# Early-stage work of a hybrid attention / Hyena / expert kernel placed on other engines: split subtractions, one modulation and half of a spectrum

## The chip, the cores and the metric

One NeuronCore of a Trainium2 chip runs the whole program. The metric is device microseconds for one execution. The kernel before took 1320.08 us (median of 3 runs, 1317.94 to 1324.70). The profile is of another execution, which took 1325.77 us.

## The reference, cut to what matters

One layer over 512 latent tokens of width 1024, with 256 context tokens:

```python
sh1, sc1, g1, sh2, sc2, g2 = adaln(c, w_mod, b_mod)          # silu(c) @ w_mod + b_mod
h  = modulate(rmsnorm(x, norm1_g), sh1, sc1)                   # h * (1 + scale) + shift
q, k, v, hy_in, cf_in = jnp.split(h @ w_in, splits, axis=-1)
hc = modulate(rmsnorm(ctx, norm1_g), csh1, csc1)               # only its k and v are used
attn = neighbourhood_attention(q, k, v, kc, vc, rpb)
hy   = hyena_mixer(hy_in, ...)      # short conv, then two gated long convolutions
cf   = conformer_conv(cf_in, ...)   # GLU, 31-tap depthwise conv, layer norm, silu
x = x + g1 * (concat([attn, hy, cf]) @ w_out)
x = x + g2 * expert_choice_ffn(modulate(rmsnorm(x, norm2_g), sh2, sc2), ...)   # 16 experts
return rmsnorm(x, final_norm_g)
```

The long convolutions of Hyena need filter spectra. The filters come from a small sine network over the 512 positions, and depend on no token:

```python
h = jnp.sin(fr * (z @ w1 + b1)); h = jnp.sin(fr * (h @ w2 + b2))
h = (h @ w3).reshape(L, 2, HY_ORDER, D_HY) * exp(-t * rate)
k_spec = jnp.fft.rfft(concat([fwd, 0, reversed(bwd[1:])]), axis=0)
```

The experts' weights are 384 MB of the 458 MB that the kernel moves.

## The kernel before, in words

**Buffers.** Large data lives in 24 buffers of 128 x 2048 floats, taken with `U(name)`. A counter `used` follows the program text: `free(k, keep)` and `free_only(k)` lower it, and `pump(keep)` (lines 72 to 74) places further loads from one long list as long as `used < 24 - keep`. Each load is one DMA on SyncE's queue, in the order of that list.

**Split products.** The projections run with operands split into two parts: `hi` is the value rounded to float32r by a ScalarE copy, `lo` is the remainder from a subtraction. `mm3` (line 547) then makes three products of 512 columns: hi·hi (line 548), lo·hi or hi·lo (549 and 550). `split` (line 510) does this for a weight buffer of 2048 columns in four slices of 512: the copy on ScalarE (line 515), the subtraction on VectorE or GpSimd (line 516); `DVE_LO` (line 491) lists which slices of which weight buffer go to VectorE. The first weights, `('hy1', 0)`, are not in the list, so all four of their subtractions are GpSimd's.

**The filter.** `filt_layer` (lines 294 to 309) is one sine layer: two products, then seven VectorE operations on each half and a ScalarE sine. The last layer's weights `fw3` are split beforehand (lines 316 to 319): the 512-column part's subtraction on VectorE, the 1024-column part's on GpSimd. `filt_out` (line 356) multiplies and applies the decay.

**The spectrum.** `spectrum` (line 383) is a generator of four steps: two over the even lags (lines 389 to 398), which make KE, and two over the odd lags (lines 399 to 411), one for each half of the frequencies. A step over the odd lags has four float32 products of 512 columns (line 406, two instructions each in the trace), two ScalarE copies with a scale (407) and four VectorE operations (409, 410), which make KP and KM. When it ends it gives back three buffers (line 412).

**Modulated x.** `modulate_split` (line 494) takes the eight 128 x 512 tiles of the transposed, normalized x in two halves of four: each is scaled and shifted (line 504, VectorE), copied to `hi` (line 505, ScalarE), and after the four come the four subtractions (line 507); the string `pool` says which tiles' subtractions are GpSimd's: here tiles 3 and 7.

**Order.** Lines 531 to 543 are a block in which TensorE, ScalarE and VectorE keep the order of the program text. A string spells it out: `a` is a step of adaln group 0 (eight steps of products with w_mod, then the row's copy, then transposes and the making of `A1` and `B1`), `F` filt_out, `s` a step of the spectrum, `T` a step of the transposes of x, `W` the split of the first projection weights, `h` and `M` the steps of modulate_split. Everything outside the block, projections, Hyena, conformer convolution, is put in order by a planner at build time, which simulates the engines from costs of its own and takes ready work in order of the program text; there the string at line 823 (`.` is one k of a projection: three products; other letters are steps beside it) gives the text order, which the planner may depart from. PSUM tiles of `psA` are four in number; the spectrum's steps and the projections both use them.

Of the kernel before, what the change touches and what calls it, by code (L numbers as in the profile page):

```python
# [9 lines left out]
FT = mybir.dt.float32  # L10
# [3 lines left out]
AF = mybir.ActivationFunctionType  # L14
OP = mybir.AluOpType
# [35 lines left out]
def hybrid_kernel(ctx: ExitStack, tc: tile.TileContext, a, out: bass.AP):  # L51
    nc = tc.nc
# [12 lines left out]
    def U(name, dt=FT):  # L65
        used[0] += 1
        assert used[0] <= NU, name
        return big.tile([128, 2048], dt, name=name, tag="U")
# [14 lines left out]
    def psA(name="psA"):  # L83
        return psum.tile([128, 512], FT, name=name, tag="A", bufs=4)
# [36 lines left out]
    A1 = small.tile([128, 2, 8], FT, name="A1")  # L121
    B1 = small.tile([128, 2, 8], FT, name="B1")
# [69 lines left out]
    v512 = lambda t: t.rearrange("p (k n) -> p k n", n=512)  # L192
# [93 lines left out]
    fw3 = take("fw3")  # L286
# [7 lines left out]
    def filt_layer(dst, m, w, rhs, b):  # L294

        ps, arg, n = psA("pF"), W("arg")[m], W("nper")[m]
        hs = [slice(0, 256), slice(256, 512)]
        for h in hs:
            mm(ps[m, h], w, rhs[:, h], start=True, stop=True)
        for h in hs:  # L300
            x_, n_ = arg[:, h], n[:, h]
            nc.vector.tensor_scalar(x_, ps[m, h], b[m], ffr[m], op0=OP.add, op1=OP.mult)
            nc.vector.tensor_scalar(n_, x_, 1.0 / TWO_PI, MAGIC, op0=OP.mult, op1=OP.add)
            nc.vector.tensor_scalar(n_, n_, MAGIC, None, op0=OP.subtract)

            for cst in (C_HI, C_LO):
                nc.vector.scalar_tensor_tensor(x_, n_, -cst, x_, op0=OP.mult, op1=OP.add)
            nc.vector.tensor_scalar(x_, x_, 3.1415925, -3.1415925, op0=OP.min, op1=OP.max)
            nc.scalar.activation(dst[m, h], x_, AF.Sin)


    fsd = fw3[:, 1024:2048]
    nc.gpsimd.tensor_add(fsd[:, 0:512], fw3[:, 0:512], fw3[:, 512:1024])
    nc.gpsimd.tensor_sub(fsd[:, 512:1024], fw3[:, 512:1024], fw3[:, 0:512])
    fw3s = [U("fw3s", FR) for _ in range(2)]
    for n, src in ((0, fsd), (1, fw3[:, 0:512])):
        w = src.shape[1]
        nc.scalar.activation(fw3s[n][:, 0:w], src, AF.Copy)
        (nc.vector if n else nc.gpsimd).tensor_sub(fw3s[n][:, 1024:1024 + w], src, fw3s[n][:, 0:w].bitcast(FT))
    h1 = W("h1")  # L320
    h2f = W("h2f")
    filt_layer(h1, slice(64, 128), p1[0:33, P1["fw1"]], dz[0:33, 1024:1536], fb1)
    filt_layer(h2f, slice(0, 128), dz[64:128, 1024:1152], h1[64:128], fb2)

    fst = U("fst", FR)
    h2s = fst[:, 0:512]
# [5 lines left out]
    hr = [U("hr0"), U("hr1")]  # L332
# [155 lines left out]

    ADA_KEEP = [7, 4, 2, 0]
    KEEP = {'hy1': 8, 'hy0': 7, 'cf': 10, 'q': 8, 'v': 7}  # L490
    DVE_LO = {('q', 0): (0, 2), ('q', 1): (1, 3), ('k', 1): (0, 1), ('k', 0): (2, 3), ('cf', 1): (0, 1), ('hy0', 1): (2, 3), ('cf', 0): (1, 3), ('hy0', 0): (0, 2)}
    ADA = [(4, 0), (4, 4), (2, 8), (2, 10)]

    def modulate_split(src, n, v, name, pool="01010101"):

        nu = (8 * n) // 2048
        hi = [U(name + "h", FR) for _ in range(nu)]
        lo = [U(name + "l", FR) for _ in range(nu)]
        per = 2048 // n
        at = lambda t, k: t[k // per].rearrange("p (k n) -> p k n", n=n)[:, k % per]  # L500
        yield (lambda k: at(hi, k)), (lambda k: at(lo, k))
        for h in range(2):
            for k in range(4 * h, 4 * h + 4):
                nc.vector.tensor_scalar(src(k), src(k), A1[:, v, k:k + 1], B1[:, v, k:k + 1], op0=OP.mult, op1=OP.add)
                nc.scalar.activation(at(hi, k), src(k), AF.Copy)  # L505
            for k in range(4 * h, 4 * h + 4):
                (nc.gpsimd if pool[k] == "1" else nc.vector).tensor_sub(at(lo, k), src(k), at(hi, k).bitcast(FT))  # L507
            yield

    def split(raw, keep, dve=()):  # L510
        hi = U("wh", FR)
        lo = U("wl", FR)
        for i in range(4):
            s = slice(i * 512, (i + 1) * 512)
            nc.scalar.activation(hi[:, s], raw[:, s], AF.Copy)  # L515
            (nc.vector if i in dve else nc.gpsimd).tensor_sub(lo[:, s], raw[:, s], hi[:, s].bitcast(FT))  # L516
        free(1, keep)
        return hi, lo
# [5 lines left out]
    def next_split():  # L524
        c, u = splits.popleft()
        presplit[c, u] = split(take(("win", c, u)), KEEP[c], DVE_LO.get((c, u), ()))

    hmod = modulate_split(lambda k: v512(hr[k // 4])[:, k % 4], 512, 0, "h", "00010001")
    ada0, spec, xt = adaln(0), spectrum(), x_transposed()
    E_ = mybir.EngineType  # L530
    with tc.manual_schedule(engines={E_.PE, E_.Activation, E_.DVE}):
        for w in "aFaasTsaTaTsTaaaaaWhMMs":
            if w == "F":
                filt_out()
            elif w == "W":
                next_split()
            elif w == "h":
                hh, hl = next(hmod)
            else:
                next({"a": ada0, "s": spec, "T": xt, "M": hmod}[w], None)  # L540
        for g in (xt, spec, ada0, hmod):
            for _ in g:
                pass
    free_only(2)
# [225 lines left out]
    def finish(*gens):  # L770
        for g in gens:
            for _ in g:
                pass
# [35 lines left out]
    side = {"h": hyena(), "m": adaln(1), "n": adaln(2), "c": conv_cf(), "x": ctx_prep()}  # L809
    side["s"] = (next_split() for _ in range(9))  # L810

    def projections():
        for c in "hy1 hy0 cf q v".split():
            yield from {"hy1": lambda: project("hy1", 2, lambda m, ps: evac_hy(m + 4, ps)), "hy0": lambda: project("hy0", 4, evac_hy),
                        "cf": lambda: project("cf", 4, evac_cf, [2, 3, 0, 1]), "q": lambda: project("q", 4, evac_q),
                        "v": lambda: project("v", 4, evac_v, ctx_part=ctx_v)}[c]()


    side["."] = projections()
    with ExitStack() as ordered:  # L820
        if False:
            ordered.enter_context(tc.manual_schedule(engines={E_.PE}))
        for w in "......s.............h............hh.......m...hm..h...h....m..m..h...h..h...h...m....hh..........h.m...mm..hh...n.h.h....h..c....m..xcnh..n..hh..m....c....c..n..c.sxn.m....c.c.c........c..c..x..c.....cc.....c........cccccccccccc":
            next(side[w], None)
        finish(side["."], *[side[w] for w in "hmncx"])
    finish(ln_cf())
    vblk = lambda c: vv[:, c // 16] if c % 16 == 0 else vo[:, c // 16]

# [25 lines left out]
    for u in range(2):  # L854
        parts.append([t.rearrange("p (k n) -> p k n", n=512) for t in split(take(("win", "k", u)), 2, DVE_LO.get(("k", u), ()))])
    fetch_bias(0)
# [353 lines left out]
    for m in marks[8 + 1:]:  # L1210
        w = mm(pw[:, 0:320], ident, xblk(0)[:, 0:320], start=True, stop=True)
# [158 lines left out]
    sd, v, r0, t, rs = (small_t(i, 1) for i in ("rv", "rt", "mx", "rv", "r1"))  # L1370
# [102 lines left out]
```

## Time and profile before

| | |
|---|---|
| median of 3 runs | 1320.08 us (1317.94 to 1324.70) |
| profiled execution | 1325.77 us, span 1324.0 us |
| busy: TensorE, VectorE, ScalarE, GpSimd | 1247.9, 512.2, 223.7, 155.2 us |
| mean granted TensorE clock | 0.988 |
| moved by DMA | 458 MB, mean 346 GB/s |

The span is read in four parts: the start up to the first projection products (0 to about 54 us), the projections with Hyena and the convolution (to 221 us), the rest of the projections with attention, output and routing (to about 390 us), and the experts. Busy shares are means over all of them.

### The profile page before, as it was taken

To read this page: it belongs to the slowest core of one execution; us is meant where nothing else is said; L and a number is where in the kernel's file an instruction comes from. 1 tells how busy PE (TensorE), PEld (TensorE's weight loads), DVE (VectorE), ACT (ScalarE), POOL (GpSimd) and SP (SyncE) were. 2 spreads that over 40 slices of the span, in tenths; PEclk is the share of its full clock that TensorE was granted. 3 is DMA by queue.
4 is the path that set the end of the run, shared out by engine and by line. 5 is a ranking of instruction groups with operands and counts; after the bars stand their busy time and mean duration, and the time that the engine had idled before them with its cause. 6 is when DMAs were issued, how large, how long until landed. Compare 5 with 4: busy or idle time off the path is not lost.

```text
span 1324.0 us, 14793 instructions
## 1 busy us (share of the span) xinstructions
PE 1247.9 (94%) x5916; PEld 566.1 (43%) x5916; DVE 512.2 (39%) x1034; ACT 223.7 (17%) x480; POOL 155.2 (12%) x166
## 2 busy tenths in 40 slices
PE   5899988999889999999999999999999999999996
PEld 2577667866634333333333333333333333333332
DVE  6878998788570121222212123121211212121232
ACT  3542232345410010101101011010101001010111
POOL 1343443556210000000000000000000000000000
PEclk9999998999989999999999999999999999999999
DMA  9944026532488999999999999999999999999997
GB/s 349 382 170 187 21 68 180 206 110 96 148 362 355 419 420 419 420 419 419 420 420 419 420 419 420 420 419 420 419 420 420 419 420 419 420 420 420 419 419 296
DMA packets 72979, 457.99 MB, mean 346 GB/s; under 512 B 7364, under 2 KB 9228, under 8 KB 21710
## 3 DMA queue, kind: packets, MB, share of 16 engines
q1 hardware_dynamic: 71662, 453.64, 84.4%
q0 software_dynamic: 912, 3.06, 0.8%
q8 instruction: 46, 0.75, 0.2%
q10 hardware_dynamic: 336, 0.35, 0.1%
q14 instruction: 23, 0.19, 0.0%
HBM read 453.87 MB, written 2.36 MB: 345 GB/s over the span
## 4 chain that ended last, share of the span: by engine, by line
PE 50%; DMA 33%; DVE 13%; issue 2%; ACT 2%; POOL 0%; POOLq 0%; SPq 0%; ACTq 0%; DVEq 0%
DMA ld<-in_w_dram 32%; PE pa L1309 18%; PE py L1349 8%; DVE glu L590 4%; PE pZ L1202 3%; PE pG L1182 2%; PE pa L1310 1%; PE pP L550 1%; PE pP L549 1%; PE pP L548 1%; PE pX L548 1%; PE pS L932 1%; DMA out_dram<-acc 1%; PE pO L963 1%; PE pX L549 1%
## 5 line engine op out<-in xcount | busy, mean ns | idle before, releaser
L1310 PE MATMUL pa<-ld,xh 128*64 128x512 f32 x1024 | 465.0, 599 | 13.3 <-DMA ld<-in_w_dram 13.3
L1309 PE MATMUL pa<-ld,xh 128*64 128x512 f32 x1024 | 467.2, 599 | 0.2 <-DVE xh L1062 0.2
L1349 PE MATMUL py<-ld,xh 128*64 128x512 f32 x1024 | 224.8, 596 | 1.0 <-DMA ld<-in_w_dram 1.0
L1309 PEld LDWEIGHTS pa<-ld,xh 128*64 128x64 f32 x1024 | 132.2, 137 | 215.2 <-issue 207.0
L1205 DVE TENSOR_TENSOR acc<-acc,pZ 128x512 f32<-128x512 f32 x112 | 73.2, 685 | 286.3 <-PE pZ L1202 285.8
L1310 PEld LDWEIGHTS pa<-ld,xh 128*64 128x64 f32 x1024 | 132.7, 137 | 87.9 <-issue 56.6
L1349 PEld LDWEIGHTS py<-ld,xh 128*64 128x64 f32 x1024 | 72.2, 138 | 141.9 <-issue 136.6
L1377 POOL DMA_INDIRECT out_dram<-yg,rwA x1 | 1.1, 1112 | 931.2 <-DVE yg L1376 931.2
L1060 ACT ACTIVATE xh<-pT,B,A 128x64 f32<-128x64 f32 (+1 forms) x60 | 24.4, 406 | 447.8 <-PE pT L1190 337.1
L1353 DVE SCALAR_TENSOR_TENSOR yg<-py,rwA,g1bc 128x512 f32<-128x512 f32 x16 | 12.0, 751 | 211.5 <-PE py L1349 211.5
L1202 PE MATMUL pZ<-yg,oh 64*128 64x512 f32 x240 | 83.2, 640 | 3.0 <-DVE acc L1205 2.3
L516 POOL TENSOR_TENSOR wl<-ld,wh 128x512 fp32r<-128x512 f32 x44 | 65.0, 1506 | 79.2 <-ACT wh L515 60.5
L548 PE MATMUL pP<-hh,wh 128*128 128x512 f32 x144 | 58.3, 406 | 1.2 <-ACT hh L505 1.2
L549 PE MATMUL pP<-hl,wh 128*128 128x512 f32 x144 | 57.0, 397 | 1.5 <-DVE hl L507 1.5
L550 PE MATMUL pP<-hh,wl 128*128 128x512 f32 x144 | 56.4, 398 | 1.1 <-DVE wl L516 1.1
L590 DVE SCALAR_TENSOR_TENSOR glu<-glu,p 128x512 f32<-128x512 f32 x60 | 55.3, 922 | 1.2
L1336 PE MATMUL pT<-c,au 128*128 128x128 f32 x256 | 48.1, 316 | 6.2 <-DVE xh L1339 2.2
L1182 PE MATMUL pG<-ld,ohg 128*64 128x512 f32 x224 | 52.5, 592 | 0.0
L103 ACT ACTIVATE xg<-pG 128x512 f32<-128x512 f32 x7 | 4.2, 598 | 275.0 <-PE pG L1182 275.0
L1062 DVE TENSOR_SCALAR xh<-pT,A,B 128x64 f32<-128x64 f32 (+1 forms) x60 | 20.6, 344 | 76.1 <-ACT xh L1060 28.5
L1202 PEld LDWEIGHTS pZ<-yg,oh 64*128 64x128 f32 x240 | 22.1, 184 | 63.2 <-issue 37.3
L1336 PEld LDWEIGHTS pT<-c,au 128*128 128x128 f32 x256 | 36.1, 209 | 26.9 <-DVE acc L1205 12.5
(342 smaller groups left out, 1349.8 us busy)
## 6 DMA issues: line engine op xcount, KB each, us to landing
ld<-in_w_dram SPq DMA_DIRECT2D x384, 1024.0 KB, 19.9
ld<-in_w_mod_dram SPq DMA_DIRECT2D x24, 1024.0 KB, 14.7
ld<-in_w_in_dram SPq DMA_DIRECT2D x11, 1024.0 KB, 7.5
ld<-in_w_out_dram SPq DMA_DIRECT2D x4, 1024.0 KB, 11.9
ld<-in_x_dram SPq DMA_DIRECT2D x2, 1024.0 KB, 12.0
ld<-in_x_dram SPq DMA_DIRECT2D x4, 512.0 KB, 6.6
out_dram<-acc SPq DMA_DIRECT2D x4, 512.0 KB, 16.8
g<-in_rpb_dram POOLq DMA_DIRECT2D x8, 244.5 KB, 4.6
```

The source lines that it names most:

```text
L516: (nc.vector if i in dve else nc.gpsimd).tensor_sub(lo[:, s], raw[:, s], hi[:, s].bitcast(FT))
L548: mm(ps, l[0], r[0], start=start, stop=False)
L549: mm(ps, l[0], r[1], start=False, stop=False)
L550: return mm(ps, l[1], r[0], start=False, stop=stop)
L590: nc.vector.scalar_tensor_tensor(yc[i], glt[i][:, j:j + 512], cw[:, i, j:j + 1], yc[i], op0=OP.mult, op1=OP.add)
L1182: mm(pg[64 * h:64 * h + 64], g[:, 64 * b:64 * b + 64], xblk(b)[:, 512 * h:512 * h + 512], start=(b == 0), stop=(b == 3))
L1202: mm(ps[h], oh[pr, 128 * c:128 * c + 128], yg[pr], start=True, stop=True)
L1205: nc.vector.tensor_add(ablk(c)[:, s], (ablk if e else xblk)(c)[:, s], ps[h])
L1309: mm(pa[f][0:64], xT[:, k, cs], w1[:, s], start=(k == 0), stop=(k == 7))
L1310: mm(pa[f][64:128], xT[:, k, cs], w3[:, s], start=(k == 0), stop=(k == 7))
L1336: nc.tensor.transpose(p[:, i * 128:(i + 1) * 128], au[f][:, c:c + 255:2], ident)
L1349: mm(py[64 * h:64 * h + 64], hT[:, f], w2[:, i * 1024 + 512 * h:i * 1024 + 512 * h + 512], start=(f == 0), stop=(f == 15))
```

## The change

Four edits. The two subtractions of the filter split both go to VectorE, and stand after the two sine layers in the text instead of ahead of them, the 512-column one first. The four subtractions of `('hy1', 0)` go to VectorE; they lie inside the hand-ordered block (`W`). Tiles 1, 3, 5 and 7 of x are scaled and shifted by ScalarE; all eight subtractions of x go to VectorE. The two spectrum steps over the odd lags leave the hand-ordered block and become steps `k` beside the first projection products, with their release of three buffers.

```diff
     for n, src in ((0, fsd), (1, fw3[:, 0:512])):
         nc.scalar.activation(fw3s[n][:, 0:w], src, AF.Copy)
-        (nc.vector if n else nc.gpsimd).tensor_sub(fw3s[n][:, 1024:1024 + w], src, fw3s[n][:, 0:w].bitcast(FT))
     filt_layer(h1, ...)
     filt_layer(h2f, ...)
+    for n, src in ((1, fw3[:, 0:512]), (0, fsd)):
+        w = src.shape[1]
+        nc.vector.tensor_sub(fw3s[n][:, 1024:1024 + w], src, fw3s[n][:, 0:w].bitcast(FT))
...
-    DVE_LO = {('q', 0): (0, 2), ...}
+    DVE_LO = {('hy1', 0): (0, 1, 2, 3), ('q', 0): (0, 2), ...}
...
-                nc.vector.tensor_scalar(src(k), src(k), A1[:, v, k:k + 1], B1[:, v, k:k + 1], op0=OP.mult, op1=OP.add)
+                if v == 0 and k % 2:
+                    nc.scalar.activation(src(k), src(k), AF.Identity, scale=A1[:, v, k:k + 1], bias=B1[:, v, k:k + 1])
+                else:
+                    nc.vector.tensor_scalar(src(k), src(k), A1[:, v, k:k + 1], B1[:, v, k:k + 1], op0=OP.mult, op1=OP.add)
                 nc.scalar.activation(at(hi, k), src(k), AF.Copy)
...
-    hmod = modulate_split(lambda k: v512(hr[k // 4])[:, k % 4], 512, 0, "h", "00010001")
+    hmod = modulate_split(lambda k: v512(hr[k // 4])[:, k % 4], 512, 0, "h", "00000000")
...
-        for w in "aFaasTsaTaTsTaaaaaWhMMs":
+        for w in "aFaasaTsTaTTaaaaaWhMM":
...
-        for g in (xt, spec, ada0, hmod):
+        for g in (xt, ada0, hmod):
...
+    side["k"] = spec
-        for w in "......s.............h............hh....
+        for w in ".k.kk....s.............h............hh....
```

## Rows read from the trace of the kernel before

**Rows 1.** Windows by stage: busy (count) PE, PEld, DVE, ACT, POOL; granted clock; DMA
```profile
64.00:124.00 60.00, 58.45 (x296) 43.64 (x295) 47.09 (x66) 24.31 (x37) 25.09 (x16) 1.00 0.45 161
124.00:221.00 97.00, 86.59 (x424) 62.09 (x423) 95.76 (x133) 26.37 (x51) 43.53 (x34) 0.97 0.32 96
221.00:390.00 169.00, 156.49 (x1018) 110.55 (x1017) 124.41 (x330) 67.12 (x162) 68.58 (x101) 0.97 0.50 185
390.00:1324.00 934.00, 899.85 (x3978) 325.79 (x3978) 197.24 (x415) 78.55 (x186) 1.11 (x1) 0.99 0.99 411
```

**Rows 2.** The chain that ended last, by line, from the page
```profile
DMA ld<-in_w_dram 32%; PE pa L1309 18%; PE py L1349 8%; DVE glu L590 4%; PE pZ L1202 3%; PE pG L1182 2%; PE pa L1310 1%; PE pP L550 1%; PE pP L549 1%; PE pP L548 1%; PE pX L548 1%; PE pS L932 1%; DMA out_dram<-acc 1%; PE pO L963 1%; PE pX L549 1%
```

**Rows 3.** Timeline of VectorE, second sine layer: start, busy, operation, count [idle before]
```profile
14.31 2.63 DVE L304 TENSOR_SCALAR nper<-nper 128x256 f32<-128x256 f32 x2
...
17.87 0.68 DVE L319 TENSOR_TENSOR fw3s<-ld,fw3s 128x512 fp32r<-128x512 f32 x1
...
18.80 0.48 DVE L308 TENSOR_SCALAR arg<-arg 128x256 f32<-128x256 f32 x2
20.54 0.69 DVE L328 TENSOR_TENSOR fst<-h2f,fst 64x512 fp32r<-64x512 f32 x1 [1.25 <-ACT fst L327]
```

**Rows 4.** Timeline of GpSimd, the filter split and the first projection split
```profile
14.14 2.44 POOL L319 TENSOR_TENSOR fw3s<-ld,fw3s 128x1024 fp32r<-128x1024 f32 x1 [1.17 <-ACT fw3s L318]
46.89 5.14 POOL L516 TENSOR_TENSOR wl<-ld,wh 128x512 fp32r<-128x512 f32 x4 [30.30 <-ACT wh L515]
```

**Rows 5.** Timeline of TensorE, from filt_out to the first projection products
```profile
21.28 1.01 PE L360 MATMUL pF<-fw3s,fst 128*1 128x512 f32 x2 [6.51 <-DVE fst L328]
...
38.46 1.88 PE L406 MATMUL pK<-sm,ld 128*128 128x512 f32 x4
...
46.34 0.66 PE L455 MATMUL pT<-c,mrow 128*128 128x128 f32 x4 [0.72 <-ACT mrow L437]
...
51.62 0.73 PE L548 MATMUL pP<-hh,wh 128*128 128x512 f32 x2 [1.19 <-ACT hh L505]
53.89 0.50 PE L549 MATMUL pP<-hl,wh 128*128 128x512 f32 x1 [1.53 <-DVE hl L507]
```

**Rows 6.** Timeline of VectorE, from A1 and B1 to the spectrum's last step
```profile
47.26 0.93 DVE L466 COPY B<-mT 128x8 f32<-128x8 f32 x1
...
49.41 3.82 DVE L504 TENSOR_SCALAR hr<-hr,A,B 128x512 f32<-128x512 f32 x4
53.15 1.88 DVE L507 TENSOR_TENSOR hl<-hr,hh 128x512 fp32r<-128x512 f32 x3
...
59.89 0.75 DVE L409 SCALAR_TENSOR_TENSOR KP<-pK,c,sn 128x512 f32<-128x512 f32 x1 [0.24 <-ACT sn L407]
```

**Rows 7.** Timeline of ScalarE: transposes' copy, weight copies, an Identity with scale and bias
```profile
36.23 1.13 ACT L103 ACTIVATE hr<-pT 128x512 f32<-128x512 f32 x1 [0.96 <-PE pT L343]
...
46.19 2.18 ACT L515 ACTIVATE wh<-ld 128x512 fp32r<-128x512 f32 x4
...
64.98 0.82 ACT L638 ACTIVATE hz<-u,p 128x512 f32<-128x512 f32 x1
```

**Rows 8.** SyncE's loads issued 20 to 30 us: issue ns, first and last start; landing
```profile
L162 SPq DMA_DIRECT2D ld<-in_w_in_dram x2: 379/5880/11382, 20.3 to 22.8; - x2
...
DMA to landing us min/median/max: 22.3/22.3/22.3
```

**Rows 9.** Timeline of TensorE, first Hyena transposes of each order
```profile
74.69 1.03 PE L666 MATMUL pT<-c,fold 128*128 128x128 f32 x8
...
121.83 0.27 PE L666 MATMUL pT<-c,fold 128*128 128x128 f32 x1
```

**Rows 10.** Timeline of TensorE, where the convolution ends
```profile
220.68 2.07 PE L598 MATMUL pL<-glu,stat 128*128 128x512 f32 x2 [3.89 <-DVE glu L590]
```

**Rows 11.** Windows of 5 us with a lower granted clock (columns as in rows 1)
```profile
175.00:180.00 5.00, 5.00 (x22) 4.11 (x20) 5.00 (x6) 3.08 (x6) 5.00 (x4) 0.66 0.23 89
...
220.00:225.00 5.00, 4.32 (x10) 2.90 (x11) 4.97 (x12) 0.77 (x2) 0.00 (x0) 0.50 1.04 337
```

More of the change, by code (lines that the diff above doesn't have):

```diff
@@ L490, in hybrid_kernel @@
     KEEP = {'hy1': 8, 'hy0': 7, 'cf': 10, 'q': 8, 'v': 7}
-    DVE_LO = {('q', 0): (0, 2), ('q', 1): (1, 3), ('k', 1): (0, 1), ('k', 0): (2, 3), ('cf', 1): (0, 1), ('hy0', 1): (2, 3), ('cf', 0): (1, 3), ('hy0', 0): (0, 2)}
+    DVE_LO = {('hy1', 0): (0, 1, 2, 3), ('q', 0): (0, 2), ('q', 1): (1, 3), ('k', 1): (0, 1), ('k', 0): (2, 3), ('cf', 1): (0, 1), ('hy0', 1): (2, 3), ('cf', 0): (1, 3), ('hy0', 0): (0, 2)}
     ADA = [(4, 0), (4, 4), (2, 8), (2, 10)]
@@ L822, in hybrid_kernel @@
             ordered.enter_context(tc.manual_schedule(engines={E_.PE}))
-        for w in "......s.............h............hh.......m...hm..h...h....m..m..h...h..h...h...m....hh..........h.m...mm..hh...n.h.h....h..c....m..xcnh..n..hh..m....c....c..n..c.sxn.m....c.c.c........c..c..x..c.....cc.....c........cccccccccccc":
+        for w in ".k.kk....s.............h............hh.......m...hm..h...h....m..m..h...h..h...h...m....hh..........h.m...mm..hh...n.h.h....h..c....m..xcnh..n..hh..m....c....c..n..c.sxn.m....c.c.c........c..c..x..c.....cc.....c........cccccccccccc":
             next(side[w], None)
-        finish(side["."], *[side[w] for w in "hmncx"])
+        finish(side["."], *[side[w] for w in "khmncx"])
     finish(ln_cf())
```

## The prediction

> **What bounds the kernel now.** I read the windows by stage first, then the chain of waits, then the timelines of the first 65 us engine by engine. The windows show a different limit in each stage [rows 1]. From 390 us to the end the DMA engines are 99% busy at 411 GB/s and TensorE is busy for 900 of 934 us: the experts' weights stream through, and nothing of the change lies there. From 124 to 221 us VectorE is busy for 95.8 of 97 us; this is the 31-tap convolution with the second half of Hyena. From 64 to 124 us TensorE is busy for 58.5 of 60 us, and so it is nearly all the time from 221 to 390 us. The chain of waits agrees: expert loads and products, then the convolution's line 590, then projection products [rows 2]. The stages follow each other without slack, so a microsecond won before the first projection products should move the convolution, the attention, the first expert loads and the end by about a microsecond. The question is only how much earlier TensorE gets through the block that starts with filt_out at 21.28 us and ends with the projection hy1.
>
> **The filter split.** The 1024-column subtraction on GpSimd runs from 14.14 to 16.58 us [rows 4]. In that time two VectorE operations of line 304 take 2.63 us, where two of the same kind and shape (line 308) take 0.48: 2.15 us lost in the chain that TensorE waits for (6.51 us idle before filt_out) [rows 3, 5]. The 512-column subtraction on VectorE adds about 0.6 in the middle of the same chain. After the change both are gone from there, and come behind it: one of 512 columns and one of 1024, for which no VectorE row stands; three of 512 take 1.88 us [rows 6], so 0.63 and, as two, 1.25, together 1.88. VectorE idles 1.25 us before line 328, for the sine and the copy [rows 3]; that hides 1.25 and 0.6 sticks out. Sum: -2.15 - 0.6 + 0.6 = -2.15. Bounds: -2.75 if nothing sticks out; -0.9 if the planner puts all 1.88 into the chain ahead of the sine (-2.15 - 0.6 + 1.88). I take -2.1, because VectorE has nothing else to do in that wait. The queue behind them holds line 328 and then filt_out's decays, which wait for products in any case.
>
> **The spectrum's first odd step.** It leaves the place ahead of the last adaln products. Its eight instructions take 3.44 us there (38.46 to 41.90, the transposes follow at once) [rows 5]. The adaln row ends 2.1 + 3.4 us earlier, less a new wait: two steps `T` now stand side by side, and the second needs the PSUM tiles which the first one's copies hold for 1.13 us [rows 7], part of it beside the first one's own transposes: 0 to 1.1, I take 0.7. So the adaln transposes come at 46.34 - 2.1 - 3.4 + 0.7 = 41.5 us and end by 42.1. The last w_mod load stands just ahead of the first projection weights in the queue; those were issued at 20.3 us, the next load at 22.8, and the one landing time shown is 22.3 us [rows 8]. If it is the first one's, the weights land at 42.6; if the second's, that one lands at 45.1 and the weights ahead of it 1.05 MB earlier, at 411 GB/s [rows 1] 42.5. The w_mod before them lands so at about 40. That is just in time, and no more than this can be won at this place.
>
> **From A1 and B1 to the first products.** Before, GpSimd's four subtractions (46.89 to 52.03) [rows 4] lie beside VectorE's small copies, one of which takes 0.93 us for eight columns, and beside four modulations of 3.82 us [rows 6]; the first remainder is ready at 53.77. After, GpSimd is silent, but VectorE has the four weight subtractions ahead of the modulations. They follow four ScalarE copies of 2.18 us [rows 7], which start when the weights land: 42.6 + 2.2 + 0.6 = 45.4. Then one modulation (0.6), the copy to hi (0.6), the remainder (0.6): 47.2 us, and from there VectorE (4 modulations and 8 remainders of 0.6) and ScalarE (8 copies of 0.55, 4 Identities of 0.82 [rows 7]) need about 1 us for each tile, below the 1.37 us of TensorE's six products for it. Moving four modulations to ScalarE costs ScalarE 3.3 us and VectorE gains 2.4; neither is late, so I cost it at nothing. Were TensorE to take a tile at a time for one output only, 0.68 us each, it would cost up to 8 x 0.3 = 2.6.
>
> **The odd steps beside the projection.** Their 16 instructions (7.0 us of TensorE) [rows 5], four ScalarE copies and eight VectorE operations of 0.75 [rows 6] are now the planner's. Their inputs are ready long before, and TensorE has nothing else between 42.1 and 47.2. Rows show that the planner slips single instructions of another step between projection products: one of eight transposes stands alone at 121.83 [rows 9]. So I expect the odd products in that gap, to 49.1 us, with the projection right behind, all tiles fed. Before, TensorE idled 1.19 + 1.53 = 2.72 us there [rows 5]; these go. Against it stands PSUM: two odd steps hold all four `psA` tiles, and the projection gets its first only when VectorE has worked off a step (4 x 0.75) between the modulations, which I reckon at 50.5 to 51; 0 to 1.6 us idle, I take 0.8. No load moves with the step, but the three buffers come back later in the text, and the three loads placed at the block's end (two of w_mod, the inverse-transform weights) move behind the next split and hy1. If they go out when the odd products end at 49.1 and take 22.3 us, they land at 71.4; Hyena's first transposes were at 74.69 [rows 9], 71.4 by this forecast. I cost that at nothing; each microsecond later would be one on Hyena.
>
> By the Trainium skill (TensorE: Matmul & The Clock Gate, the section on clock oscillation) idle gaps of TensorE bring its clock to half, which then makes the products after the gap cost double. The trace agrees at one gap: 3.89 us of idle time before 220.68 [rows 10], then a granted clock of 0.50 in the next 5 us [rows 11]. By that rule a gap from 42.1 to 47.2 that stays unfilled costs more than its length; this is a rival below.
>
> **Sum.** -2.1 - 2.72 + 0.7 + 0.8 = -3.3 us (the first odd step itself is no gain: it is still done, only later). With the bounds: -2.75 - 2.72 = -5.5 at best, -0.9 - 2.72 + 1.1 + 1.6 + 2.6 = +1.7 at worst. On the profiled execution 1325.77 - 3.3 = 1322.5 us (span 1320.7); it lies 5.7 above the median of 1320.08, so for the median 1316.8.
>
> **Rivals.**
> *The gap stays open.* The planner keeps the text's order (three projection products first, then `k`), TensorE waits from 42.1 to 47.2: -2.1 - 2.72 + 0.7 + 5.1 = +1.0. The clock at 0.50 over 5 us, as after the gap at 220 us [rows 11], costs 2.5 more: +3.5, 1323.6. For it: the text puts one `.` ahead. Against: the planner's fillings above.
> *The gains are eaten later.* The planner orders the 64 to 221 us anew; VectorE has 1.2 us to spare in the convolution's 97 [rows 1], so anything put in there costs fully. About 0: 1320.
> *Slower: PSUM held until the modulations are over.* If VectorE does the odd steps' operations after the modulations, as before (59.89, behind all of them [rows 6]), the tiles come free at 45.4 + 10.2 (the modulations' length before, 49.41 to 59.6) + 3.0 = 58.6. TensorE idles from 49.1, 9.5 us, and then half a clock costs 2.5: -2.1 - 2.72 + 0.7 + 9.5 + 2.5 = +7.9, 1328. It decides from about 7 us of idle time on. Against: VectorE has gaps between the tiles, which wait for ScalarE's copies.
> *Faster: the clock.* The falls at 175 and 220 us (0.66 and 0.50 over 5 us [rows 11], worth 1.7 + 2.5) follow waits whose length hangs on the planner's order. Were both gone: -3.3 - 4.2 = -7.5, 1312.6. Nothing in the change aims at them.
>
> **How the numbers follow.** Forecast 0.42, open gap 0.17, eaten 0.13, PSUM 0.12, clock 0.16. I call faster or slower what is beyond 0.5% (6.6 us), about what a measurement of this kernel can tell. Faster: most of the clock case and the forecast's far end with an early median, 0.14 + 0.09 = 0.23. Slower: most of the PSUM case and a little of the open gap, 0.10 + 0.03 = 0.13. The rest, 0.64, is within. The range goes from 1308 (the clock case with the filter and PSUM at their best ends, 1320.08 - 9.7, less 2 for the spread of the runs of before) to 1327 (nearly the PSUM case).
>
> **What would show it.** Line 304's pair at about 0.5 us and filt_out at about 19.1; adaln's transposes at 41 to 42; line 406 on TensorE between those and the first line 548, which starts at 49 to 51; the second hy1 tile's evacuation 2 to 5 us earlier; the convolution's end (line 598) 3 us earlier, and the same 3 at the first expert loads. The prediction is wrong if line 406 stands behind the first projection products, if TensorE idles over 3 us between 42 and 52, or if the 3 us are seen at 65 us and not at 221.

## The result, and the profile after

The changed kernel took 1331.98 us (median of 7 runs, 1330.74 to 1334.38) beside 1320.36 us for the kernel before (7 runs on the same chip, 1317.94 to 1326.12). The ratio of the runs is 1.0071 with a 95% interval from 1.0051 to 1.0091: slower by 9.4 us, and outside the predicted range. The profiled execution took 1331.47 us (span 1329.7, mean granted clock 0.988); the one of before lies 5.4 us above its median, so the two profiles differ by 5.7 us only, and the medians by 11.6.

The windows by stage come first, with the columns of [rows 1], in the same order, the last one to the end of the span:

```profile
64.00:124.00 60.00, 55.41 (x276) 40.84 (x275) 45.51 (x64) 20.07 (x29) 22.22 (x14) 0.97 0.44 147
124.00:221.00 97.00, 87.27 (x411) 62.27 (x410) 90.38 (x126) 28.48 (x54) 39.82 (x31) 0.96 0.25 83
221.00:390.00 169.00, 156.63 (x1048) 113.75 (x1046) 119.92 (x305) 69.26 (x167) 72.86 (x105) 0.99 0.50 173
390.00:1330.00 940.00, 904.56 (x3997) 332.00 (x3996) 204.84 (x448) 78.54 (x187) 2.17 (x2) 0.99 1.00 413
```

From 64 to 124 us TensorE is busy for 55.41 us where it was 58.45, with 20 instructions fewer, and the clock fell to 0.97 where it was 1.00. VectorE's full stage does not fill its window any more (90.38 instead of 95.76), because it starts later. The last stage streams weights at the same rate as before. So the loss is looked for ahead of about 130 us. TensorE's timeline there (start, busy, operation, count, in brackets the idle time before and who ended it) has two long waits:

```profile
43.21 0.66 PE L457 MATMUL pT<-c,mrow 128*128 128x128 f32 x4 [0.72 <-ACT mrow L439]
48.16 0.80 PE L554 MATMUL pP<-hh,wh 128*128 128x512 f32 x1 [4.29 <-ACT hh L510]
48.75 3.19 PE L408 MATMUL pK<-sm,ld 128*128 128x512 f32 x4
51.78 1.45 PE L408 MATMUL pK<-df,ld 128*128 128x512 f32 x3
...
107.07 0.38 PE L704 MATMUL pH<-ld,Y 128*128 128x128 f32 x2
...
112.98 1.22 PE L704 MATMUL pH<-ld,Y 128*128 128x128 f32 x4 [4.59 <-DVE Y L694]
```

and the windows of 5 us around them show the granted clock between its two levels, 1.2 and 2.4 GHz (full speed is 1.00):

```profile
45.00:50.00 5.00, 1.84 (x3) 1.17 (x4) 4.04 (x8) 2.72 (x6) 0.00 (x0) 0.80 1.01 401
50.00:55.00 5.00, 5.00 (x12) 2.10 (x10) 3.49 (x7) 4.31 (x8) 0.00 (x0) 0.86 1.04 425
...
110.00:115.00 5.00, 2.02 (x7) 1.82 (x8) 4.97 (x13) 0.00 (x0) 1.45 (x1) 0.78 0.00 0
115.00:120.00 5.00, 5.00 (x34) 4.56 (x33) 2.14 (x6) 0.77 (x2) 0.00 (x0) 0.88 0.00 0
```

The first wait is the gap between the adaln transposes and the first projection product: one product, then at once the odd steps (line 408 here, 406 before). By the time the second tile of the projection hy1 leaves PSUM (ScalarE's copy, before and after), 2.1 us are lost:

```profile
65.70 1.09 ACT L636 ACTIVATE u<-pP 128x512 f32<-128x512 f32 x1
...
67.84 1.11 ACT L642 ACTIVATE u<-pP 128x512 f32<-128x512 f32 x1 [0.50 <-PE pP L556]
```

The second wait stands in front of Hyena's inverse products (line 704; 698 before), which take Y, the filtered spectrum that VectorE makes, back to positions. In the kernel before it was there too, but short:

```profile
108.73 0.39 PE L550 MATMUL pP<-hh,wl 128*128 128x512 f32 x1
110.60 1.16 PE L698 MATMUL pH<-ld,Y 128*128 128x128 f32 x8 [1.49 <-DVE Y L688]
```

A TensorE account from filt_out to the last product of the first sigmoid's tile: 96.0 us before (21.28 to 117.28) with 5.35 us of waits and no loss of clock; 104.27 after (20.37 to 124.64) with 10.32 us of waits, and four windows of 5 us whose clocks (0.80, 0.86, 0.78, 0.88) lack 3.4 us. Both stretches hold 443 TensorE instructions. 4.97 + 3.4 = 8.37 accounts for the 8.27 that the stretch is longer. What follows is late by as much or a little more: the first glu operation (the convolution's input gate) comes at 131.55 instead of 123.52 us, the convolution ends at 230.4 instead of 219.9, the first expert product comes at 401.0 instead of 392.7. At the end the two profiles lie only 5.7 us apart, as the one of before has a fall of the clock from 385 to 400 us (0.67, 0.50, 0.81, together 5.1 us) that this one of after has not.

The place of the inverse products in TensorE's queue is the plan's. Counted in projection products ahead of them:

```
             first Hyena products   sixteen inverse products of the first order
before       96                     177, 186, 195 x4, 197 x10
after        113                    177, 181 x2, 186 x13
```

The trace shows what such a place costs: TensorE idles for 4.59 us in front of the inverse products at 112.98 us, with projection products queued behind them that run without a wait from 108 us on where the inverse products stand later (run 6 below). VectorE makes Y, and from its product with KM to the next Y it works off more in the plan after. Before:

```profile
105.22 1.28 DVE L685 TENSOR_TENSOR t<-pH,KM 128x512 f32<-128x512 f32 x2
...
107.86 1.29 DVE L687 TENSOR_TENSOR t<-t 128x512 f32<-128x512 f32 x2
109.18 1.37 DVE L688 TENSOR_TENSOR Y<-t 128x256 f32<-128x256 f32 x1
```

After:

```profile
103.39 1.28 DVE L691 TENSOR_TENSOR t<-pH,KM 128x512 f32<-128x512 f32 x2
104.59 2.38 DVE L522 TENSOR_TENSOR wl<-ld,wh 128x512 fp32r<-128x512 f32 x2
106.89 3.44 DVE L693 TENSOR_TENSOR t<-t 128x512 f32<-128x512 f32 x2
110.25 1.74 DVE L646 SCALAR_TENSOR_TENSOR hx<-u,p,hx 128x511 f32<-128x511 f32 x1
111.92 0.68 DVE L693 TENSOR_TENSOR t<-t 128x512 f32<-128x512 f32 x1
112.52 0.41 DVE L694 TENSOR_TENSOR Y<-t 128x256 f32<-128x256 f32 x1
```

### The profile page after: what moved, and what is told of

It reads as the page before. It is cut to its first block, busy times and chain, and to the rows that moved or that the text cites. A ratio compares the mean times of both kernels' runs of the same rounds, so it can differ in the third digit from the quotient of the medians.

```text
span 1329.7 us, 14785 instructions
## 1 busy us (share of the span) xinstructions
PE 1249.3 (94%) x5916; PEld 571.2 (43%) x5916; DVE 504.9 (38%) x1037; ACT 226.5 (17%) x484; POOL 142.7 (11%) x159
## 4 chain that ended last, share of the span: by engine, by line
DMA 45%; PE 39%; DVE 12%; issue 2%; ACT 1%; POOL 0%; POOLq 0%; SPq 0%; ACTq 0%; DVEq 0%
DMA ld<-in_w_dram 44%; PE pa L1316 12%; PE py L1356 5%; DVE glu L596 4%; PE pZ L1209 2%; PE pP L554 2%; PE pP L555 2%; PE pP L556 2%; PE pa L1317 1%; PE pG L1189 1%; DMA out_dram<-acc 1%; PE pO L970 1%; PE pX L554 1%; PE pS L939 1%; PE pX L555 1%
## 5 line engine op out<-in xcount | busy, mean ns | idle before, releaser
L522 POOL TENSOR_TENSOR wl<-ld,wh 128x512 fp32r<-128x512 f32 x40 | 60.0, 1524 | 93.7 <-ACT wh L521 90.2
```

## The experiments

Seventeen runs. Ratios are to the kernel before on the same chip, with their 95% intervals; "wait" is TensorE's waiting for VectorE in front of the first order's inverse products (for Y; in run 11, 1.2 us of it are put down to line 687, which makes Y's input).

| run | us | ratio | wait, us |
|---|---|---|---|
| after | 1331.98 | 1.0071 (1.0051 to 1.0091) | 4.6 |
| 1 spectrum back at its old places | 1325.79 | 1.0025 (1.0009 to 1.0042) | 2.2 |
| 2 the spectrum's move alone | 1332.57 | 1.0081 (1.0059 to 1.0104) | 4.6 |
| 3 first gap filled | 1330.96 | 1.0071 (1.0050 to 1.0093) | 4.6 |
| 4 first Hyena products earlier | 1331.34 | 1.0075 (1.0053 to 1.0096) | 3.0 |
| 5 = 1 and 4 | 1327.36 | 1.0034 (1.0016 to 1.0051) | 3.9 |
| 6 inverse products later | 1325.46 | 1.0020 (1.0006 to 1.0033) | 1.3 |
| 7 = 3, 4 and 6 | 1324.81 | 1.0017 (0.9999 to 1.0035) | 0.4 |
| 8 = 1, 4 and 6 | 1323.10 | 0.9992 (0.9980 to 1.0003) | 1.3 |
| 9 before, inverse products early | 1326.01 | 1.0022 (1.0001 to 1.0042) | 2.6 |
| 10 before, inverse products later | 1321.66 | 0.9981 (0.9965 to 0.9998) | 1.1 |
| 11 before, filter edit alone | 1325.11 | 1.0008 (0.9987 to 1.0029) | 1.8 |
| 12 = 10 and 11 | 1323.82 | 0.9997 (0.9980 to 1.0015) | 2.3 |
| 13 = 6, gap kept busy, too long | 1334.13 | 1.0103 (1.0071 to 1.0136) | 1.3 |
| 14 = 6, gap kept busy | 1322.73 | 1.0013 (0.9995 to 1.0030) | 1.0 |
| 15 = 10 again | 1320.26 | 0.9986 (0.9971 to 1.0001) | 1.1 |
| 16, 17 before and after, profiled again | 1326.37, 1335.43 | one execution each | 1.5, 4.6 |

### Which edit it is: runs 1 and 2

Run 1 undoes the spectrum's move alone, run 2 makes it alone, on the kernel before:

```diff
-        for w in "aFaasaTsTaTTaaaaaWhMM":
+        for w in "aFaasaTsTaTsTaaaaaWhMMs":
...
-        for w in ".k.kk....s....
+        for w in "......s....
```

> The changed kernel with the spectrum's odd steps back at their old places in the hand-ordered block; the filter split, the first weights' split, the remainders of x and its modulation stay as changed. In the planned order the first Hyena products (L683 there) still stand behind 116 projection products (changed kernel 113, before 96). Gap theory (the whole loss comes from the spectrum's move: TensorE's open gap of 4.3 us, the half clock after it, and what follows): 1316 to 1321 us. Order theory (most of the loss is the planner's later place for the first Hyena products, which any shift of the early times brings): 1323 to 1328. Split theory (the subtractions moved to VectorE delay the first products, the spectrum is innocent): 1329 to 1333.

> The kernel before with the spectrum's move alone (both strings, the steps k). Its first Hyena products stand behind 113 projection products. Gap theory: 1329 to 1334, as slow as the changed kernel or a little slower, since the filter's gain is missing. Order theory: the same, 1328 to 1333. Split theory: 1319 to 1322.

Run 2 is as slow as the whole change, so the move alone is enough for the loss. Run 1 keeps about a third of it (3.3 us): the three edits of splits and modulation cost something by themselves, where they were to win, and nothing on top of the move. Both times agree with the order theory.

### Two places where it could cost: runs 3 and 4

Run 3 puts the first odd step's four products by hand into the gap, its ScalarE copies and VectorE work behind the modulations. Run 4 binds thirteen tile steps of the projections (the expectation says twelve) behind Hyena's first four products, so that these stand behind 96 products again.

```diff
                 for j in (2, 3):
                     mm(pr[ri], dft[:, j, c:c + 128], v512(rhs)[:, j], start=(j == 2), stop=(j == 3))
+            yield
+            for ri in range(2):
                 nc.scalar.activation(sn[ri], pr[ri], AF.Copy, scale=si)
...
-        for w in "aFaasaTsTaTTaaaaaWhMM":
+        for w in "aFaasaTsTaTTaaaaasWhMMs":
```

> The changed kernel with the first odd step cut in two: its four products stand by hand right behind the adaln transposes, in TensorE's gap, its ScalarE and VectorE part behind the modulations; the second odd step stays beside the projection. Both theories: the gap before the first projection product (4.3 us) under 1.5 us and the second hy1 evacuation at 62 to 65 us instead of 67.8. Gap theory: total 1320 to 1325. Order theory (first Hyena products still behind 113): 1326 to 1330, since their place, counted in products, has not changed.

```diff
-        mm(ps, l[0], r[0], start=start, stop=False)
+        first = mm(ps, l[0], r[0], start=start, stop=False)
+        if hold:
+            hold[0] += 1
+            if hold[0] > 1:
+                after(first, hold[1])
```

> The changed kernel with twelve k-steps of the projection bound behind the first four Hyena products, so that these stand behind 96 projection products as before. The gap stays. Gap theory: 1329 to 1333, nothing won. Order theory: first Hyena product at 79 to 80 us instead of 83.3, first gated tile (line 589's counterpart) 3 to 5 us earlier than 131.6, total 1323 to 1328.

Run 4 did what it should at its place (first Hyena products at 79.3 instead of 83.3 us) and ends where the changed kernel ends, so the late start of Hyena is not what costs. Run 3 closed the gap (0.85 us are left, clock 1.00 behind it), but the second hy1 tile came at 67.58 us, where 62 to 65 was expected and 67.84 is the changed kernel's. What was won in the gap was lost again within 12 us: 1.80 us of waiting for an odd step's last operations on VectorE (KM), which hold the PSUM tiles, and 1.0 us in short waits for modulated tiles:

```profile
60.07 1.98 PE L408 MATMUL pK<-df,ld 128*128 128x512 f32 x4 [1.80 <-DVE KM L413]
```

So run 3 does not decide what the gap costs; it shows that filling it with an odd step wins nothing. In both runs the wait in front of the inverse products stayed, at 4.6 and 3.0 us, with a clock of 0.57 and 0.77 in the window from 110 us. Waits of TensorE from 40 to 125 us in run 3 (us in total, times, longest):

```profile
PE pH L706 <- DVE Y L696: 4.6, 1, 4.6
PE pK L408 <- DVE KM L413: 1.8, 1, 1.8
PE pP L556 <- ACT hh L512: 1.2, 2, 0.9
```

### The inverse products' place: runs 5 to 8

In the text string, the two Hyena steps that hold the inverse products move from behind the 59th and the 62nd tile step to behind the 66th (`h` moves, nothing else):

```diff
-  ..h...h....m..m..h...h..h...h...m....hh....
+  ..h...h....m..m..h...h........m.hh...hh....
```

> The changed kernel, with the two steps of Hyena's text that hold the sixteen inverse products (line 704) placed behind the 66th tile step of the projections instead of behind the 59th and the 62nd. Stall theory (the 4.6 us that TensorE waits at 113 us in front of these products, and the half clock behind them, are what is lost in this stretch): that wait is under 1 us, the clock from 110 to 120 us is 1.00, the glu starts at 125 to 127 us instead of 131.6, and the end is 1325 to 1328. VectorE theory (VectorE is late with the second hy1 tile and with Hyena's adds beside GpSimd, and TensorE's wait is only where it shows): another wait takes its place, the glu starts at 130 to 132, and the end is 1330 to 1334.

> The changed kernel with the three corrections together: the first odd step's products by hand ahead of the modulations, twelve tile steps held behind Hyena's first four products, the inverse products behind the 66th tile step. Stall theory: neither wait is left, the glu starts at 121 to 124 us, and the end is 1317 to 1323, level with the kernel before. VectorE theory: the glu starts at 128 us or later, and the end is 1327 to 1332.

> The spectrum at its old places, the edits of splits and modulation kept, and twelve tile steps held behind Hyena's first four products. The spectrum at its old places without the hold came out at 1325.8 with Hyena's first products at 82.8 us (76.3 in the kernel before). If their lateness is what those edits cost: they start at 77 to 79 us and the end is 1319 to 1323. If it is the additional work on VectorE: 1324 to 1328.

> The same as the run before (spectrum at its old places, splits and modulation as changed, twelve tile steps held), with the inverse products behind the 66th tile step as well. Stall theory: the wait of 1.8 us in front of the inverse products goes too, the glu starts at 121 to 123 us, and the end is 1316 to 1321. VectorE theory: the glu starts at 126 to 129, the end is 1324 to 1328.

Moving two letters (run 6) takes 1.0071 to 1.0020, 6.7 us (by the two intervals 3.5 to 9.9). All sixteen then stand behind 198 products, and the first glu operation comes at 125.9 us, as the stall theory had it; the wait of 1.3 us is a little over its 1 us. VectorE makes Y no earlier in run 6 than in the changed kernel: the two operations below start at 113.06 and 115.19 us, where the same two start at 112.52 and 114.64 after. So it is the place in TensorE's queue that was won, and not Y. VectorE, run 6:

```profile
113.06 0.41 DVE L694 TENSOR_TENSOR Y<-t 128x256 f32<-128x256 f32 x1
...
115.19 0.42 DVE L694 TENSOR_TENSOR Y<-t 128x256 f32<-128x256 f32 x1
```

TensorE from 108 to 122 us in run 6:

```profile
113.50 0.83 PE L704 MATMUL pH<-ld,Y 128*128 128x128 f32 x6
115.66 3.17 PE L704 MATMUL pH<-ld,Y 128*128 128x128 f32 x26 [1.32 <-DVE Y L694]
```

with a clock of 1.00 from 110 to 120 us. The same step takes run 5 (1.0034) to run 8 (0.9992), 4.3 us by the medians of one chip. 3.3 us of wait and 1.7 us of clock are 5.0 of the 6.7; the traces show where more may have come from. After, SyncE's next loads of w_in wait for Y and then for the inverse products:

```profile
SPq L162 <- DVE Y L695: 12.7, 1, 12.7
...
SPq L162 <- PE pH L704: 3.8, 1, 3.8
```

They are issued from 119.29 us; before and in run 6, where the profile puts no wait of theirs down to Y, from 108.27 and 110.92. After, the weights land so late that VectorE idles for 6.12 us, and the convolution's first operation stands behind their split. VectorE, after:

```profile
129.22 0.69 DVE L522 TENSOR_TENSOR wl<-ld,wh 128x512 fp32r<-128x512 f32 x1 [6.12 <-ACT wh L521]
130.26 1.37 DVE L522 TENSOR_TENSOR wl<-ld,wh 128x512 fp32r<-128x512 f32 x1 [0.35 <-ACT wh L521]
131.55 1.09 DVE L589 TENSOR_TENSOR glu<-pP,sig 128x512 f32<-128x512 f32 x1
```

In run 6 the sigmoid comes 3.3 us earlier than after (122.65 for 125.95) and the glu 5.6. The share of this was not tried by itself, and is not shown.

Run 5 does not show what it was built for: with the hold Hyena's first products still start at 82.45 us (82.77 in run 1), where 77 to 79 was expected. Run 7 missed the stall theory's 1317 to 1323 by 2 us: with the inverse products in place, the filled gap and the earlier Hyena products add nothing that can be told (1.0017 beside 1.0020). Run 8 shows no gain either over the kernel before, with all of the change but the move. In both the glu comes at about 126 us, 2 us or more behind the stall theory's times, and run 8's 1323.10 lies between the two theories. In both profiled executions filt_out came 1.4 us later than in the changed kernel's (21.8 and 21.7 us for 20.4); what else delays the glu stays open.

### The same in the kernel before: runs 9 to 12 and 15

> The kernel before, nothing of the change in it, with up to thirty tile steps of the projections bound behind Hyena's sixteen inverse products, so that these stand where the changed kernel has them: behind 186 products (ten of them stand behind 197 in the kernel before). Stall theory: TensorE waits 4 to 6 us in front of them instead of 1.5, the granted clock falls behind the wait, the glu starts 4 to 7 us later than in the kernel before, and the end is 3 to 6 us above it. If these products' place is not what costs in the changed kernel (its VectorE work is): Y is ready in time here, the wait stays under 2.5 us, and the end is within 2 us of the kernel before.

> The kernel before with the two steps of the inverse products behind the 66th tile step. Its wait there is only 1.5 us, without a fall of the clock. Stall theory: little to win, 0 to 2 us below the kernel before. If the later place itself shortens the stretch behind it (Hyena's second order, attention) whatever the wait: 3 us or more below.

> The kernel before with the two filter subtractions alone as in the change (both on VectorE, behind the sine layers in the text). The prediction gave them 2.1 us; the changed kernel's filt_out came 0.9 us earlier, because both stand inside the sine chain in the plan. If a microsecond there is one at the end: 0.5 to 1.5 us below the kernel before. If it is lost on the way: within 0.5 us of it.

> The filter subtractions as in the run before, and the inverse products behind the 66th tile step: the candidate to beat both kernels. If the two add up: 1.5 to 3.5 us below the kernel before. If the weight loads bound what is left: within 1 us of it.

> The kernel before with the inverse products later, again, in five rounds: three gave 0.9981 with an interval from 0.9965 to 0.9998. If the gain is real: 0.997 to 0.999. If it was the scatter of the kernel before (1317.5 to 1328.1 us): 0.999 to 1.001.

Run 9 binds thirty tile steps behind the last inverse product (`after(first, y_last)`), nothing of the change in it. It waits 2.6 us, less than the 4 to 6 expected, as Y is ready earlier there; the clock falls to 0.87 and 0.79 behind it, the first glu operation comes 5.2 us later (128.75 for 123.52), and the end is 2.9 us above the kernel before. That is the stall theory's direction, with the end just under its 3 to 6 us; in this execution the clock had also fallen behind the first products (0.73 and 0.59 from 50 to 60 us), so not all of the glu's delay is the place's. Run 10 is 2.5 us below the kernel before, its repeat 1.8; together the only version with an interval below 1, by about 2 us, and in the repeat the interval touches 1. Runs 11 and 12 show no gain by the filter edit.

### The wait and the clock behind it: runs 13, 14, 16 and 17

Products that nobody reads, between the adaln transposes and the first projection product, on top of run 6:

```diff
+    def keep_busy():
+        d, s = busy[0]
+        ps = psY("pD")
+        for i in range(18):
+            mm(ps, d[:, 2, 0:128], s[:, 2], start=(i == 0), stop=(i == 17))
...
-        for w in "aFaasaTsTaTTaaaaaWhMM":
+        for w in "aFaasaTsTaTTaaaaaDWhMM":
```

> The changed kernel with the inverse products later, and eighteen products of 128x512 whose result nobody reads put on TensorE between the last adaln transposes and the first projection product (4.1 us by 0.23 us each), so that the wait of 4.3 us stays as it is but TensorE works through it. If the fall of the granted clock behind the wait is what the wait costs beyond itself: the clock from 45 to 55 us is 1.00 instead of 0.85 and 0.81, the second hy1 tile's evacuation comes 1 to 1.7 us earlier, the glu starts at 124 to 125 us instead of 125.9, and the end is 1 to 2 us lower (1323 to 1325 beside a kernel before at 1322.5). If the clock falls whatever TensorE does there: nothing moves.

Mis-sized: these are float32 products of two instructions of 0.43 us each, so eighteen took 15.6 us. It became a dose test: the first projection product 10.6 us later than in run 6 (59.23 for 48.6), the glu and the convolution's end 9.4 later each, the last expert product 8.2 (1322.0 for 1313.8), and the ratio up by 0.0083, 11 us. A microsecond lost ahead of the projections is about a microsecond at the end.

> The run with eighteen unread products again, with five: each of them took 0.87 us, not 0.23, so that eighteen took 15.6 us and pushed the first projection product from 48.6 to 59.2 us; five take 4.3, the length of the wait. If the fall of the clock is a cost beside the wait: the clock from 45 to 55 us is 1.00, the second hy1 tile's evacuation comes 1 to 1.7 us earlier than in the run with the inverse products later alone, and the end is 1 to 2 us below that run's (0.2% above the kernel before). If the clock's fall is made up for later anyway: the clock is 1.00 and the end the same within 1 us.

With five, TensorE's timeline and windows of run 14:

```profile
43.28 0.66 PE L466 MATMUL pT<-c,mrow 128*128 128x128 f32 x4 [0.72 <-ACT mrow L448]
43.78 4.46 PE L391 MATMUL pD<-sm,ld 128*128 128x512 f32 x10
48.23 0.51 PE L565 MATMUL pP<-hh,wh 128*128 128x512 f32 x1
```

```profile
45.00:50.00 5.00, 5.00 (x13) 2.14 (x12) 4.04 (x8) 2.72 (x6) 0.00 (x0) 1.00 1.02 403
50.00:55.00 5.00, 5.00 (x16) 2.63 (x15) 3.58 (x7) 4.33 (x9) 0.00 (x0) 1.00 1.04 426
```

The clock stays at 1.00. From the adaln transposes to the second hy1 tile's evacuation it is 23.2 us (43.28 to 66.48) where run 6 needs 24.7 (43.60 to 68.33). That 1.5 us is near the 1.7 that the clock lacked there in run 6 (0.85 and 0.81), but the plan placed the last odd pair earlier too (behind 16 products, not 22), and the two are not told apart. At the end it is 0.9 us by the ratios, with intervals that overlap.

> The kernel before, unchanged, for a second profiled execution. In two variants of it with the same two waits of 1.2 and 1.5 us in front of the first projection products the clock fell to 0.6 to 0.85 behind them, in two others and in the first profile it did not. If that is a matter of the execution and not of the plan, the same kernel's second profile may show a fall at 50 to 60 us or at 110 to 120, and its total lies then 2 to 4 us above that of an execution without one. If it is a matter of the plan: the clock is 1.00 there again.

> The changed kernel, unchanged, for a second profiled execution. If the two long waits (4.3 us at 48, 4.6 us at 113) always bring the clock down: it reads 0.75 to 0.9 again from 45 to 55 and from 110 to 120 us. If that is a matter of the execution: one of the two is missing, and the total is 1 to 2 us lower.

The kernel before, profiled again, has the same waits of 1.19 and 1.53 us as in [rows 5], but this time the clock fell behind them:

```profile
50.00:55.00 5.00, 2.93 (x7) 2.11 (x8) 5.00 (x7) 2.15 (x4) 2.94 (x2) 0.74 1.04 423
55.00:60.00 5.00, 5.00 (x22) 4.06 (x22) 4.75 (x9) 4.59 (x9) 2.23 (x3) 0.92 1.02 419
```

So with short waits the fall belongs to the execution, not to the plan. The changed kernel's long waits brought it both times, the second time deeper (0.72 and 0.59 in the windows from 45 us, 0.71 and 0.61 from 110), and that execution took 1335.43 us. Between the two executions of the changed kernel the time differs by 4.0 us, and the clocks of all 5 us windows, summed, lack 3.9 us more in the second.

## Why the prediction was wrong, step by step

Two steps failed, one on each side of 68 us. Run 6 tells them apart: with the inverse products' place put right, the second hy1 tile comes 2.6 us later than before (68.33 for 65.70), the first glu operation 2.4, and the end is 2.6 later by the ratio. So about 2 to 3 us were lost early, where 3.3 were to be won, and about 6.7 behind.

**No term for the stretch behind (the step that put the time outside the range).** The sum ended at the first projection products: what is won there moves everything. The dose test bears the rule out. But the rival *gains are eaten later*, put at "about 0", had a price: the planner ordered 64 to 124 us anew, with the inverse products ahead of projection products that used to cover the wait for Y. Of the 9.4 us, 6.7 go with that place: some 5.0 as wait and clock at 113 us; for the rest the late w_in load is a candidate that was not tried by itself. That the same stretch already had a wait of 1.5 us in front of these products stood in the trace of before; it was not asked what would happen to it.

**The odd steps in the gap (the step that had the sign wrong).** The sum let 2.72 us of waits go and took 0.8 for PSUM, with "all tiles fed". Text order won instead: one product, then the odd steps, the rival *the gap stays open* (chance 0.17, forecast 1323.6, with three products ahead). Its wait measured 4.29 us for a forecast 5.1, its clock 1.7 (0.80 and 0.86) for 2.5. The reason given against it, that the planner slips single instructions of another step between products, told nothing about work that the text puts behind a product which is not ready. The second hy1 tile, forecast 2 to 5 us earlier, came 2.1 later. Nor does the forecast come true with an odd step in the gap: in run 3 the tile comes at 67.58, as PSUM costs 1.80 us for the 0.8, the tiles are not all fed (1.0 us), and the other odd step's 3.4 us of products still stand among the projection's. How the early loss divides between these stays open.

The Trainium skill (TensorE: Matmul & The Clock Gate, the section on oscillation) warns of clock falls behind gaps of TensorE. This case agrees at each of the waits of 2.6 to 4.6 us that these runs have between 40 and 125 us; behind the waits of 1.2 and 1.5 us the clock fell in one execution (run 16) and not in another, and run 14 shows the other side, a gap worked through without a fall.

**The filter split.** Forecast -2.1; measured -0.9 against the first profile (filt_out at 20.37 for 21.28), the worse bound. The planner put both subtractions into the sine chain. Line 304's pair did fall to 0.49. VectorE, second sine layer, after, against [rows 3]:

```profile
14.41 0.49 DVE L304 TENSOR_SCALAR nper<-nper 128x256 f32<-128x256 f32 x2
14.81 0.42 DVE L307 SCALAR_TENSOR_TENSOR arg<-nper,arg 128x256 f32<-128x256 f32 x1
15.15 1.22 DVE L325 TENSOR_TENSOR fw3s<-ld,fw3s 128x1024 fp32r<-128x1024 f32 x1
...
16.96 0.68 DVE L325 TENSOR_TENSOR fw3s<-ld,fw3s 128x512 fp32r<-128x512 f32 x1
```

And the 2.15 us that were to go were not always there: in the second profile of before the same pair takes 0.49 us beside GpSimd's subtraction, which takes 4.81 instead of 2.44 [rows 4], and filt_out comes at 19.93:

```profile
14.28 0.49 DVE L304 TENSOR_SCALAR nper<-nper 128x256 f32<-128x256 f32 x2
...
19.93 1.01 PE L360 MATMUL pF<-fw3s,fst 128*1 128x512 f32 x2 [5.08 <-DVE fst L328]
```

Against that execution the edit loses 0.4 us. In six profiles of kernels with the old split, VectorE's pair was slow in three (before, runs 2 and 10) and GpSimd's subtraction in three (runs 9, 15 and 16). A term was taken from one execution of a contention that goes either way.

**The adaln row.** Forecast 41.5, measured 43.21. The missing 1.2 us of the filter are most of it; what remains, about 1.2 us where 0.7 was taken, is the adjoining steps' (`T`, with waits of 0.27 and 0.45 us for their copies): 46.34 - 0.9 - 3.4 + 1.2 = 43.2.

**From A1 and B1 to the first products.** The small copies, 0.93 us before beside GpSimd [rows 6], took 0.17, and the weights were there. But the tiles ran at ScalarE's pace: with four Identities and eight copies it, not VectorE, is waited for (0.2 to 0.7 us ahead of several remainders). "Neither is late" was wrong by little.

**PSUM.** Right in kind: the last odd pair stands behind 22 products (59.98 us), and the rival *PSUM held*, 9.5 us of idle time, did not come; with an odd step in the gap (runs 3 and 7) 1.8 us of it did. The loads that go out later were rightly put at nothing: in run 4 Hyena's first products follow its transposes at once (79.3 behind 77.7 us). The *clock* rival did not come either: for the falls at 175 and 220 us the changed kernel has others, at 195 to 205 and 230 to 240 us (0.82, 0.50, 0.73, 0.93), of about the same size, and 3.4 us came on top ahead of 125 us.

**The slower side.** The rival named for it (7.9 us by PSUM) came near the size by chance, through a mechanism that did not act; the one that did had no price.

## What to carry to other kernels

Where a planner orders the queues, moving work is not a local edit: list the waits that an engine already has further down its queue, and ask of each what covers it now and whether the new plan keeps that cover; here two letters of a text string gave back 6.7 of 9.4 us. A gap won early counts only up to the next wait that is set by another engine: the gap filled in run 3 was lost again at 60 us. And before a stall is entered as a gain, look whether a second profile has it.

## What the runs showed of the hardware

- The clock behind short TensorE waits varies between executions of one program: 1.00 and 0.74 in the window from 50 us behind the same 1.2 and 1.5 us of waiting. Behind each wait of 2.6 to 4.6 us between 40 and 125 us it fell; with unread products in the gap it did not.
- VectorE's tensor-scalar pair and GpSimd's 1024-column subtraction, started within 0.3 us of each other, do not share evenly: 2.63 and 2.44 us in one execution, 0.49 and 4.81 in another.
- The executions of the kernel before spread over 10 us (1317.5 to 1328.1 in 31 runs); differences of 2 us between plans need the ratio's interval beside them. The time goes with the mean granted clock of the execution: in these 31 runs 1317.5 to 1322.2 us at 0.993 and above, 1323.8 to 1328.1 at 0.988 and below.
- The clock column can read 1.00 where the products are spaced as at the lower level: before, from 22.09 to 24.22 us, behind 6.51 us of idle time, 512-column products (line 365) start 0.43 us apart, where others of that width stand at 0.23. The changed kernel has the same there, so it drops out of the comparison.

What stays open: why the planner put the inverse products earlier (its costs are not in the trace), and how the remaining 0.2% of run 6 divides between the first gap, its clock, the odd steps' products and PSUM tiles, and the edits on VectorE.
